# MLP down-projection of a float32 trunk kernel: 2x2 block products with seven multiplications instead of eight, and buffers that start at multiples of 256 bytes

## The chip, the core and the metric

The kernel runs on one core of a Trainium2 chip. A core has TensorE (PE in the profile; PEld is its weight load), VectorE (DVE), ScalarE (ACT), GpSimd (POOL) and a queue that issues transfers (SP). SBUF is its on-chip memory of 128 partitions, PSUM the eight banks (128 partitions x 512 float32) that matmuls add into. The metric is the device time of one execution in microseconds; lower is better. Before the change it is 1307.33 us, the median of three runs between 1307.11 and 1307.74.

## The reference, cut to what matters

Two residual layers (a gated position mixer, then forgetting attention), each followed by a squared-ReLU MLP, on 512 tokens of width 1024, all in float32. The change touches the MLP, which runs twice:

```python
D_MODEL = 1024; SEQ = 512; D_FF = 4 * D_MODEL
def sqrelu_mlp(h, w1, w2):
    return jnp.square(jax.nn.relu(h @ w1)) @ w2
for i in range(DEPTH):                      # DEPTH = 2
    x = x + mixer(rms_norm(x, mix_norm_g[i]))
    x = x + sqrelu_mlp(rms_norm(x, mlp_norm_g[i]), mlp_w1[i], mlp_w2[i])
```

## The kernel before, in words

The residual stream lies transposed in SBUF as eight tiles `x0` to `x7`, each 128 features x 512 tokens. A float32 operand is split into a rounded high part and the remainder (`fp32r` tiles: `wh`, `wl` of a weight, `xh`, `xl` of the normed stream, `zh`, `zl` of the hidden values), and one product is three matmuls (`mm3`, line 198): high by high, high by low, low by high. All matmuls of the page stand at line 191, the helper `mm`.

Weights come through `Stream` (line 46): 512 KB chunks of 128 x 1024, loaded by SP into one of three `raw` buffers (line 65), split by ACT (`wh`, line 75) and by DVE or, in the attention stage, POOL (`wl`, line 77), into four `wh` and four `wl` buffers. `take` (line 91) hands out the next chunk and splits three chunks further ahead. The order of the instructions on each engine is made by a scheduler from the program's order, except in the attention stage, whose matmuls are pinned.

An MLP (`mlp`, from line 397) works in eight groups of four 128-wide blocks of the 4096 hidden features. `up` (`dense_a`, line 256) makes one hidden block: 8 input blocks x 3 = 24 matmuls of 512 columns into a PSUM bank `ph`. `square` turns it into `zh`, `zl`: DVE takes the ReLU and the row scale (`r`, line 409), ACT squares (`z`, line 411) and rounds (`zh`, line 414), DVE subtracts (`zl`, line 415). `out_chunk` (line 278) then takes a 256-column chunk of `w2` for the four hidden blocks of the *previous* group: 2 output blocks x 4 x 3 = 24 matmuls of 512 columns into banks `po`, each followed by an add into `x` on DVE (line 273). So `up` and `out_chunk` alternate, 24 matmuls each, and POOL has no work in an MLP. At the end of each MLP four `out_chunk` follow each other. In the second MLP each finished `x` is stored; in the first it goes into the attention stage's norm (`Norm.block`, line 213).

Where the buffers lie: in the built program, `raw`, `wh`, `wl`, `x`, `xh`, `xl` and the gated mixer's `zh`, `zl` (`gzh`, `gzl`) start 64 bytes past a multiple of 256 in their partition, the MLP's `zh`, `zl` 192 past one, the attention stage's `oh`, `ol` 128 or 64 past one.

Of the kernel before, what the change touches and what calls it, by code (L numbers as in the profile page):

```python
# [8 lines left out]
F32 = mybir.dt.float32  # L9
F32R = mybir.dt.float32r  # L10
AF = mybir.ActivationFunctionType
ALU = mybir.AluOpType
# [4 lines left out]
P = 128  # L17
# [25 lines left out]
WARM = 20  # L43


class Stream:


    def __init__(self, nc, pool, chunks, bufs, ahead, load_ahead, halved=()):
        self.nc, self.pool, self.chunks, self.bufs = nc, pool, chunks, bufs  # L50
# [7 lines left out]

    def _load(self):
        i = self.loaded  # L60
        src = self.chunks[i]
# [5 lines left out]
        self.loaded += 1  # L67

    def _split(self):
        nc, i = self.nc, self.split  # L70
        t, n = self.raw.pop(i)
        hi = self.pool.tile([P, CHUNK_COLS], F32R, tag="wh", name=f"wh{i}", bufs=self.bufs[1])
        lo = self.pool.tile([P, CHUNK_COLS], F32R, tag="wl", name=f"wl{i}", bufs=self.bufs[1])
        for sl in self._pieces(i, n):
            nc.scalar.activation(hi[:, sl], t[:, sl], AF.Copy)  # L75
            eng = nc.gpsimd if i in self.pooled else nc.vector
            eng.tensor_tensor(lo[:, sl], t[:, sl], hi[:, sl].bitcast(F32), op=ALU.subtract)  # L77
        self.parts[i] = (hi, lo)
        self.split += 1

    def load(self, upto):
        while self.loaded < min(len(self.chunks), upto):
# [16 lines left out]
def trunk(ctx: ExitStack, tc: tile.TileContext, A, out, stages=4):  # L99
# [30 lines left out]

    def mlp_chunks(w1, w2):
        r = []
        for g in range(8):
            for m in range(4):
                r += [w1[4 * g + m], w2[g - 1, m]] if g else [w1[4 * g + m]]
        return r + [w2[7, m] for m in range(4)]

    chunks += mlp_chunks(A["m0_1"], A["m0_2"])
    lo_pool = [len(chunks)]
# [40 lines left out]
    dve.memset(mhalf, -0.5)  # L180

# [5 lines left out]
            tc.keep_in_program_order(ins)  # L187
            order["us"] += max(cols, 256) / 2400

    def mm(dst, a, b, start, stop):  # L190
        ins = pe.matmul(dst, a, b, start=start, stop=stop)  # L191
        placed(ins, dst.shape[-1])
        return ins

    def turn(dst, src):
        placed(pe.transpose(dst, src, ident[: src.shape[0], : src.shape[0]]), 256)

    def mm3(dst, ah, al, bh, bl, start, stop, pin=False):
        first = mm(dst, ah, bh, start, False)
        if pin:  # L200
            tc.keep_in_program_order(first)
        mm(dst, ah, bl, False, False)
        mm(dst, al, bh, False, stop)

    class Norm:

# [87 lines left out]
    with ExitStack() as st:  # L294
        gp = st.enter_context(tc.tile_pool(name="gp", bufs=1))

        v = [gp.tile([P, E], F32, tag=f"v{i}", name=f"v{i}") for i in range(NT)]
        bn = small.tile([P, NT, 4, 6], F32, tag="bn", name="bn")
        for g in range(4):
# [18 lines left out]
            if g == 1:  # L318
                wsT = wp.tile([P, G, P], F32, tag="raw", name="wsT", bufs=3)
                nc.sync.dma_start(wsT, A["w_sT"].rearrange("g s t -> s g t"))  # L320
                pool.affine_select(wsT, wsT, pattern=[[0, G], [1, P]], compare_op=ALU.is_ge, fill=0.0, base=0, channel_multiplier=-1)
                wsb = gp.tile([P, G, 2, P], F32R, tag="wsb", name="wsb")
                pool.tensor_scalar(wsb[:, :, 0], wsT, 1.0, None, op0=ALU.mult)
                pool.tensor_tensor(wsb[:, :, 1], wsT, wsb[:, :, 0].bitcast(F32), op=ALU.subtract)
                lngb = gp.tile([P, 2, E // P], F32, tag="lngb", name="lngb")
                nc.sync.dma_start(lngb, A["ln_gb"])
# [68 lines left out]


    def mlp(nm, done):
        with ExitStack() as st:
            mp = st.enter_context(tc.tile_pool(name="mp", bufs=2))
            prev = None  # L400
# [5 lines left out]
            def square(f, ph):  # L406
                f = f"{nm.n}_{f}"
                r = mp.tile([P, S], F32, tag="r", name=f"r{f}", bufs=2)
                dve.scalar_tensor_tensor(r, ph, 0.0, nm.rbc, op0=ALU.max, op1=ALU.mult)  # L409
                z = mp.tile([P, S], F32, tag="z", name=f"z{f}", bufs=2)  # L410
                act.activation(z, r, AF.Square)
                h = mp.tile([P, S], F32R, tag="zh", name=f"zh{f}", bufs=8)
                l = mp.tile([P, S], F32R, tag="zl", name=f"zl{f}", bufs=8)
                act.activation(h, z, AF.Copy)
                dve.tensor_tensor(l, z, h.bitcast(F32), op=ALU.subtract)
                return h, l

            for g in range(8):
                if g == 0:
                    phs = [up(0), up(1)]  # L420
                    nm.finish()
                    phs.append(up(2, True))
                    nm.spread()
                    phs.append(up(3, True))
                    z = [square(f, ph) for f, ph in enumerate(phs)]
                else:
                    z = []
                    for m in range(4):
                        z.append(square(4 * g + m, up(4 * g + m)))
                        out_chunk(m, *prev, 4, 256)  # L430
                zh, zl = ([t[q] for t in z] for q in range(2))
                prev = (zh, zl)
            out_partial(*prev, 4, 256, done)

    def store(b):
        nc.sync.dma_start(out[b * P : (b + 1) * P, :], x[b])
# [11 lines left out]

    nx3 = Norm(3)
    with ExitStack() as st:  # L450
        fp = st.enter_context(tc.tile_pool(name="fp", bufs=2))
        qkg = fp.tile([P, 2], F32, tag="qkg", name="qkg", bufs=1)
        nc.scalar.dma_start(qkg, A["qk_g"])
        qkn = fp.tile([P, 1], F32, tag="qkn", name="qkn", bufs=1)
        dve.tensor_scalar(qkn, qkg[:, 0:1], -(DH**-0.5), None, op0=ALU.mult)
        bf = fp.tile([P, H], F32, tag="bf", name="bf", bufs=1)
        nc.sync.dma_start(bf, A["b_f"].partition_broadcast(P))
        tri = fp.tile([P, P], F32, tag="tri", name="tri", bufs=1)
        pool.affine_select(tri, ones, pattern=[[1, P]], compare_op=ALU.is_ge, fill=0.0, base=0, channel_multiplier=-1)
        did = set()  # L460
# [72 lines left out]
        def project(p, values=True):  # L533
# [26 lines left out]
            ss = fp.tile([P, NT, 4], F32, tag="yss", name=f"yss{p}")  # L560
# [39 lines left out]
        def attend(p, y):  # L600
# [21 lines left out]
            for e in range(2):  # L622
# [6 lines left out]
                sm = fp.tile([P, NT], F32, tag="sm", name=f"sm{hd}")  # L629
                mn = fp.tile([P, NT], F32, tag="mn", name=f"mn{hd}")  # L630
# [16 lines left out]
                rc = fp.tile([P, NT], F32, tag="rc", name=f"rc{hd}")  # L647
# [170 lines left out]
```

## Time and profile before

| | before |
|---|---|
| median of three runs | 1307.33 us |
| the profiled execution's own time | 1307.18 us |
| its span, first to last instruction | 1305.5 us |
| PE busy | 1294.8 us (99%), 6196 matmuls |
| DVE busy | 742.0 us (57%) |
| ACT busy | 547.4 us (42%) |
| POOL busy | 309.0 us (24%) |

The profiled execution is 0.15 us below the median; 1.7 us of it lie around the span. A matmul's row in the timeline has a modelled end, so the pace of matmuls is read from one start to the next, or from the chain of work that ended last, which merges a run of them: 24 matmuls and the time to the next piece. A busy share is an average over stages; the MLPs fill about 287 to 640 us and 955 to 1302 us.

### The profile page before, as it was taken

What the parts mean: (1) busy time and instruction counts of PE and PEld (TensorE: products, weight loads), DVE (VectorE), ACT (ScalarE), POOL (GpSimd) and SP (SyncE); (2) the same over time, 40 slices, a digit from 0 to 9 for tenths busy, and PEclk for the clock granted to TensorE, in tenths of its full rate; (3) what the DMA queues carried; (4) which work ended last, traced back from release to release, by engine and by line L of the source; (5) the groups of instructions that cost most, each with busy time, mean ns of one, the idle gap of its engine ahead of it and who ended that gap; (6) DMA issues with size and microseconds to landing.
All of it is one profiled execution on the core that took longest, in us unless ns stands there. A gap on an engine that the chain in (4) does not pass through costs nothing. (4 is left out here: it accounts for less than half of the span.)

```text
span 1305.5 us, 16106 instructions
## 1 busy us (share of the span) xinstructions
PE 1294.8 (99%) x6196; PEld 1090.5 (84%) x6196; DVE 742.0 (57%) x1132; ACT 547.4 (42%) x864; POOL 309.0 (24%) x296
## 2 busy tenths in 40 slices
PE   9999999999999999999999999999999999999998
PEld 8888888888888888888899899998878888888886
DVE  7347766684444444444637777777864444444443
ACT  7234332343333333222467687787443332222231
POOL 4108523020000000000657567675320000000000
PEclk9999999999999999999999999999999999999999
DMA  7332322323333333332223222223222322333321
GB/s 243 97 111 84 87 91 86 92 90 94 95 93 97 97 97 97 97 97 93 70 87 102 82 81 78 93 67 112 82 87 92 96 97 97 97 98 97 97 81 65
DMA packets 39485, 123.87 MB, mean 95 GB/s; under 512 B 4688, under 2 KB 5728, under 8 KB 39408
## 3 DMA queue, kind: packets, MB, share of 16 engines
q1 hardware_dynamic: 39232, 122.82, 30.1%
q8 instruction: 49, 0.80, 0.2%
q14 instruction: 28, 0.23, 0.1%
q0 software_dynamic: 32, 0.02, 0.0%
q10 hardware_dynamic: 144, 0.00, 0.0%
HBM read 120.69 MB, written 2.13 MB: 94 GB/s over the span
## 5 line engine op out<-in xcount | busy, mean ns | idle before, releaser
L75 ACT ACTIVATE wh<-raw 128x1024 fp32r<-128x1024 f32 (+3 forms) x230 | 231.9, 1008 | 599.9 <-PE ph L191 264.5
L77 DVE TENSOR_TENSOR wl<-raw,wh 128x1024 fp32r<-128x1024 f32 (+1 forms) x178 | 220.6, 1240 | 78.9 <-ACT wh L75 73.4
L273 DVE TENSOR_TENSOR x<-x,po 128x512 f32<-128x512 f32 x192 | 131.0, 686 | 153.5 <-PE po L191 150.9
L191 PE MATMUL po<-zh,wl 128*128 128x512 f32 x512 | 202.2, 395 | 0.0
L191 PE MATMUL po<-zl,wh 128*128 128x512 f32 x512 | 202.0, 394 | 0.0
L191 PE MATMUL po<-zh,wh 128*128 128x512 f32 x512 | 201.8, 395 | 0.0
L191 PE MATMUL ph<-xl,wh 128*128 128x512 f32 x512 | 199.5, 390 | 0.7 <-DVE xl L219 0.7
L191 PE MATMUL ph<-xh,wh 128*128 128x512 f32 x512 | 199.6, 390 | 0.0
L191 PE MATMUL ph<-xh,wl 128*128 128x512 f32 x512 | 199.4, 390 | 0.0
L77 POOL TENSOR_TENSOR wl<-raw,wh 128x768 fp32r<-128x768 f32 (+3 forms) x52 | 102.4, 1970 | 398.2 <-ACT wh L75 395.7
L409 DVE SCALAR_TENSOR_TENSOR r<-ph,rbc 128x512 f32<-128x512 f32 x64 | 44.1, 692 | 187.5 <-PE ph L191 187.3
L191 PEld LDWEIGHTS po<-zl,wh 128*128 128x128 f32 x512 | 96.1, 188 | 23.2
L191 PEld LDWEIGHTS po<-zh,wl 128*128 128x128 f32 x512 | 96.1, 188 | 23.2
L191 PEld LDWEIGHTS po<-zh,wh 128*128 128x128 f32 x512 | 96.1, 188 | 22.6
L191 PEld LDWEIGHTS ph<-xl,wh 128*128 128x128 f32 x512 | 96.1, 188 | 21.6 <-DVE xl L219 1.4
L191 PEld LDWEIGHTS ph<-xh,wh 128*128 128x128 f32 x512 | 96.1, 188 | 20.7
L191 PEld LDWEIGHTS ph<-xh,wl 128*128 128x128 f32 x512 | 96.1, 188 | 20.2
L191 PE MATMUL pq<-wh,xh 128*128 128x384 f32 (+2 forms) x256 | 88.7, 347 | 0.0
L191 PE MATMUL pq<-wh,xl 128*128 128x384 f32 (+2 forms) x256 | 83.4, 326 | 0.0
L191 PE MATMUL pq<-wl,xh 128*128 128x384 f32 (+2 forms) x256 | 83.2, 325 | 0.0
L355 POOL TENSOR_SCALAR vn<-v,mv,lnr 128x128 f32<-128x128 f32 x64 | 65.1, 1029 | 57.6 <-DVE vl L359 57.5
L191 PE MATMUL pv<-wh,xh 128*128 128x512 f32 (+1 forms) x160 | 58.8, 372 | 0.0
(154 smaller groups left out, 2180.9 us busy)
## 6 DMA issues: line engine op xcount, KB each, us to landing
raw<-in_m_dram SPq DMA_DIRECT2D x128, 512.0 KB, 3.6
raw<-in_gw_u_dram SPq DMA_DIRECT2D x16, 512.0 KB, 3.5
raw<-in_gw_o_dram SPq DMA_DIRECT2D x16, 512.0 KB, 3.5
raw<-in_fw_qkv_dram SPq DMA_DIRECT2D x20, 384.0 KB, 3.0
raw<-in_gw_v_dram SPq DMA_DIRECT2D x14, 512.0 KB, 3.6
raw<-in_fw_g_dram SPq DMA_DIRECT2D x8, 512.0 KB, 3.6
cb<-cd SPq DMA_DIRECT2D x16, 256.0 KB, 3.3
raw<-in_fw_o_dram SPq DMA_DIRECT2D x8, 512.0 KB, 3.6
```

The lines of the kernel that those rows point to most:

```text
L75: nc.scalar.activation(hi[:, sl], t[:, sl], AF.Copy)
L77: eng.tensor_tensor(lo[:, sl], t[:, sl], hi[:, sl].bitcast(F32), op=ALU.subtract)
L191: ins = pe.matmul(dst, a, b, start=start, stop=stop)
L273: dve.tensor_tensor(x[b], x[b], pt, op=ALU.add)
L355: pool.tensor_scalar(vn[:, i], v[i][:, cb * P : (cb + 1) * P], mv[:, i, 0:1], lnr[:, i : i + 1], op0=ALU.subtract, op1=ALU.mult)
L409: dve.scalar_tensor_tensor(r, ph, 0.0, nm.rbc, op0=ALU.max, op1=ALU.mult)
```

## The change: seven products, and where buffers lie

The down-projection's hidden features are taken in four groups of 1024 instead of eight of 512. In a group, an output of 256 features x 512 tokens is a 2x2 block matrix: the weights are blocks A11, A12, A21, A22 (output halves by hidden halves; A11 and A21 come in the first `w2` chunk, A12 and A22 in the second) and the hidden values are blocks B11, B12, B21, B22 (hidden halves by token halves, 256 tokens each). Four sums of each are made beforehand: `_sums` makes S1 = A21 + A22, S2 = S1 - A11, S3 = A11 - A21, S4 = A12 - S2 on POOL (128x512 each), split by ACT and DVE (128x1024, twice); `squares` makes T1 = B12 - B11, T2 = B22 - T1, T3 = B22 - B12, T4 = B21 - T2 on POOL (128x256 each), and one ACT round and one DVE subtract over seven of the eight blocks (128x1792). Then come seven products of 4 x 3 matmuls of 256 columns. Their intermediate results are chained in PSUM: a bank is added into `x` by DVE, and PE then goes on adding into the same bank:

```python
product(a, a11, B11, z, True);   add(b1, late, a)
product(c, s1, T1, z, True);     add(b2, early, c)
if behind: behind()              # the previous pair's last product
product(a, s2, T2, z, False);    add(b1, early, a)
product(b, a12, B21, z, True);   add(b1, late, b)
product(c, s4, B22, z, False);   add(b1, early, c)
product(a, s3, T3, z, False);    add(b2, early, a)
# later, as `last`: product(a, a22, T4, z, False); add(b2, late, a)
```

A pair of chunks (one `down`) is thus 84 matmuls of 256 columns, where the two `out_chunk`s over the same weights were 48 of 512 columns; an MLP has 16 pairs. `add` is seven DVE adds of 128x256 for a pair. The order in an MLP is no longer one `up` and one `out_chunk` in turn:

```diff
+MLP_ORDER = [("up", 0, n) for n in range(4)]
+for _g in range(4):
+    MLP_ORDER += [("up", _g + 1, 0)] if _g < 3 else []
+    MLP_ORDER += [("down", _g, n) for n in range(4)]
+    MLP_ORDER += [("up", _g + 1, n) for n in range(1, 4)] if _g < 3 else []
...
+        if kind == "first":
+            self._parts(*(blocks(q)[:, :, 0] for q in (hi, lo, t)), eng)
...
+        s = sp.tile([P, 4, h], F32, tag="ssum", name=f"ssum{i}", bufs=1)
...
+        tt(s1, a21, a22, op=ALU.add)
+        tt(s2, s1, a11, op=ALU.subtract)
+        tt(s3, a11, a21, op=ALU.subtract)
+        tt(s4, a12, s2, op=ALU.subtract)
...
+            hi = sp.tile([P, 2, h], F32R, tag="sh", name=f"sh{i}_{q}", bufs=3)
+            lo = sp.tile([P, 2, h], F32R, tag="sl", name=f"sl{i}_{q}", bufs=3)
+            self._parts(hi, lo, s[:, 2 * q : 2 * q + 2], nc.vector)
...
+    def pad(at, words):
+
+        dve.memset(at.tile([P, words], F32, tag="pad", name="pad", bufs=1), 0.0)
...
+    pad(const, 48)
...
+            pad(mp, 32)
...
-            for g in range(8):
...
-                        z.append(square(4 * g + m, up(4 * g + m)))
-                        out_chunk(m, *prev, 4, 256)
```

Here an `up` is a pair of hidden blocks (48 matmuls of 512 columns). The `pad` tiles and small tiles that moved to pools of their own (`fs` in the attention stage, `lngb` ahead of the mixer's other tiles) put every operand of a matmul at a multiple of 256 bytes. Up to the first MLP every engine's instructions stand in the order that they had, the load of `lngb` in SP's queue too; only the memsets of the pads are new on DVE.

On PE, at the end of the second MLP's last `up` (`ph3_31` is the bank of hidden block 31), the down-projection began with hidden blocks 24 to 27, which were long done:

```order
L191 MATMUL ph3_31_10698<-xl3_7_8544,wh222_10593 128x512
L191 MATMUL ph3_31_10698<-xh3_7_8543,wl222_10594 128x512
L191 MATMUL po224_0_10739<-zh3_24_10222,wh223_10628 128x512
L191 MATMUL po224_0_10739<-zl3_24_10223,wh223_10628 128x512
L191 MATMUL po224_0_10739<-zh3_24_10222,wl223_10629 128x512
L191 MATMUL po224_0_10739<-zh3_25_10295,wh223_10628 128x512
```

Now thirty matmuls on the hidden values `zh3_3_0` and `zh3_3_1` of the same group follow `ph3_31` (banks `ca` and `cc` of pairs 0 and 1 and `cb` of pair 0); these are the last of them, and then those that need `zh3_3_2`:

```order
L243 MATMUL cc3_3_1_12134<-zh3_3_0_11287,sl223_0_12004 128x256
L243 MATMUL cc3_3_1_12134<-zh3_3_1_11825,sh223_0_12003 128x256
L243 MATMUL cc3_3_1_12134<-zl3_3_1_11826,sh223_0_12003 128x256
L243 MATMUL cc3_3_1_12134<-zh3_3_1_11825,sl223_0_12004 128x256
L243 MATMUL ca3_3_0_12017<-zh3_3_2_11900,wh220_11863 128x256
L243 MATMUL cc3_3_0_12031<-zh3_3_2_11900,sh221_0_11916 128x256
L243 MATMUL cb3_3_0_12058<-zh3_3_2_11900,wh221_11907 128x256
```

The hidden values of the group's last `up` (`zh3_3_3`, the blocks of `ph3_31`) are needed 45 matmuls behind `ph3_31`, their low part 50 behind it.

On DVE, in the middle of the first MLP, an `out_chunk` and an `up` in turn asked this of it (`po` adds, weight splits `wl`, the ReLU `r`, the hidden `zl`):

```order
L273 TENSOR_TENSOR x0_97<-x0_97,po62_0_2965 128x512
L273 TENSOR_TENSOR x1_98<-x1_98,po62_1_2979 128x512
L77 TENSOR_TENSOR wl65_2997<-raw65_2886,wh65_2996 128x1024
L409 SCALAR_TENSOR_TENSOR r1_9_3024<-ph1_9_2993,rbc1_2563 128x512
L77 TENSOR_TENSOR wl66_3035<-raw66_2921,wh66_3034 128x1024
L415 TENSOR_TENSOR zl1_9_3029<-z1_9_3026,zh1_9_3028 128x512
```

Now, between two `down`s of one group, adds for three banks of two pairs stand among splits of weights and of weight sums (`sl`):

```order
L88 TENSOR_TENSOR wl79_3749<-raw79_3597,wh79_3748 128x1024
L490 TENSOR_TENSOR x0_97<-x0_97,ca1_1_0_3665 128x256
L88 TENSOR_TENSOR sl77_1_3656<-ssum77_3646,sh77_1_3655 128x1024
L490 TENSOR_TENSOR x0_97<-x0_97,cc1_1_0_3679 128x256
L490 TENSOR_TENSOR x2_99<-x2_99,ca1_1_1_3771 128x256
L490 TENSOR_TENSOR x1_98<-x1_98,ca1_1_0_3665 128x256
L490 TENSOR_TENSOR x2_99<-x2_99,cb1_1_1_3825 128x256
L490 TENSOR_TENSOR x2_99<-x2_99,cc1_1_1_3785 128x256
L88 TENSOR_TENSOR sl79_0_3758<-ssum79_3752,sh79_0_3757 128x1024
```

An add into `x` stood behind work on other tiles before too, but PE had two more banks to go on with; now PE's next product into the same bank waits for that add.

More of the change, by code (lines that the diff above doesn't have):

```diff
@@ L43, with blocks @@
 WARM = 20
+MLP_ORDER = [("up", 0, n) for n in range(4)]
[3 more added lines that the diff above has]
+    MLP_ORDER += [("up", _g + 1, n) for n in range(1, 4)] if _g < 3 else []
+def blocks(t):
+    return t.rearrange("p (k o m) -> p k o m", k=4, o=2)
 class Stream:
     def __init__(self, nc, pool, chunks, bufs, ahead, load_ahead, halved=()):
-        self.nc, self.pool, self.chunks, self.bufs = nc, pool, chunks, bufs
+        self.nc, self.pool, self.bufs = nc, pool, bufs
+        self.chunks = [c if isinstance(c, tuple) else (c, None) for c in chunks]
+        self.sums_pool = None
         self.ahead, self.load_ahead = ahead, load_ahead
@@ L67, in _load, with _parts, _sums @@
         self.loaded += 1
+    def _parts(self, hi, lo, t, eng):
+        self.nc.scalar.activation(hi, t, AF.Copy)
+        eng.tensor_tensor(lo, t, hi.bitcast(F32), op=ALU.subtract)
     def _split(self):
         nc, i = self.nc, self.split
-        t, n = self.raw.pop(i)
+        kind = self.chunks[i][1]
+        t, n = self.raw[i] if kind == "first" else self.raw.pop(i)
         hi = self.pool.tile([P, CHUNK_COLS], F32R, tag="wh", name=f"wh{i}", bufs=self.bufs[1])
         lo = self.pool.tile([P, CHUNK_COLS], F32R, tag="wl", name=f"wl{i}", bufs=self.bufs[1])
[L74 to L77, printed above, removed]
+        eng = nc.gpsimd if i in self.pooled else nc.vector
+        if kind == "first":
+            self._parts(*(blocks(q)[:, :, 0] for q in (hi, lo, t)), eng)
+        for sl in self._pieces(i, n) if kind != "first" else []:
+            self._parts(hi[:, sl], lo[:, sl], t[:, sl], eng)
         self.parts[i] = (hi, lo)
+        if kind == "second":
+            self._sums(i, self.raw.pop(i - 1)[0], t)
         self.split += 1
+    def _sums(self, i, f, g):
+        nc, sp = self.nc, self.sums_pool
+        h = CHUNK_COLS // 2
+        a11, a12, a21, a22 = (blocks(t)[:, :, o] for o in range(2) for t in (f, g))
+        s = sp.tile([P, 4, h], F32, tag="ssum", name=f"ssum{i}", bufs=1)
+        tt = nc.gpsimd.tensor_tensor
+        s1, s2, s3, s4 = (s[:, q].rearrange("p (k m) -> p k m", m=P) for q in range(4))
+        tt(s1, a21, a22, op=ALU.add)
+        tt(s2, s1, a11, op=ALU.subtract)
+        tt(s3, a11, a21, op=ALU.subtract)
+        tt(s4, a12, s2, op=ALU.subtract)
+        made = []
+        for q in range(2):
+            hi = sp.tile([P, 2, h], F32R, tag="sh", name=f"sh{i}_{q}", bufs=3)
+            lo = sp.tile([P, 2, h], F32R, tag="sl", name=f"sl{i}_{q}", bufs=3)
+            self._parts(hi, lo, s[:, 2 * q : 2 * q + 2], nc.vector)
+            made += [tuple(t[:, e].rearrange("p (k m) -> p k m", m=P) for t in (hi, lo)) for e in range(2)]
+        self.parts[i] += (made,)
     def load(self, upto):
@@ L132, in mlp_chunks @@
         r = []
-        for g in range(8):
-            for m in range(4):
-                r += [w1[4 * g + m], w2[g - 1, m]] if g else [w1[4 * g + m]]
-        return r + [w2[7, m] for m in range(4)]
+        for kind, g, n in MLP_ORDER:
+            if kind == "up":
+                r += [w1[8 * g + n], w1[8 * g + 4 + n]]
+            else:
+                r += [(w2[2 * g, n], "first"), (w2[2 * g + 1, n], "second")]
+        return r
     chunks += mlp_chunks(A["m0_1"], A["m0_2"])
@@ L188, in placed, with mm @@
             order["us"] += max(cols, 256) / 2400
-    def mm(dst, a, b, start, stop):
-        ins = pe.matmul(dst, a, b, start=start, stop=stop)
+    def mm(dst, a, b, start, stop, more=False):
+        ins = pe.matmul(dst, a, b, start=start, stop=stop, skip_group_check=more)
         placed(ins, dst.shape[-1])
@@ L196, in turn, with mm3 @@
         placed(pe.transpose(dst, src, ident[: src.shape[0], : src.shape[0]]), 256)
-    def mm3(dst, ah, al, bh, bl, start, stop, pin=False):
-        first = mm(dst, ah, bh, start, False)
+    def mm3(dst, ah, al, bh, bl, start, stop, pin=False, more=False):
+        first = mm(dst, ah, bh, start, False, more)
         if pin:
             tc.keep_in_program_order(first)
-        mm(dst, ah, bl, False, False)
-        mm(dst, al, bh, False, stop)
+        mm(dst, ah, bl, False, False, more)
+        mm(dst, al, bh, False, stop, more)
     class Norm:
@@ L295, in trunk @@
         gp = st.enter_context(tc.tile_pool(name="gp", bufs=1))
+        lngb = gp.tile([P, 2, E // P], F32, tag="lngb", name="lngb")
+        nc.sync.dma_start(lngb, A["ln_gb"])
         v = [gp.tile([P, E], F32, tag=f"v{i}", name=f"v{i}") for i in range(NT)]
@@ L397, in mlp @@
     def mlp(nm, done):
+        HS = S // 2
+        early, late = slice(0, HS), slice(HS, S)
         with ExitStack() as st:
             mp = st.enter_context(tc.tile_pool(name="mp", bufs=2))
-            prev = None
+            ws.sums_pool = mp
+            pad(mp, 32)
             def up(f, pin=False):
@@ L404, in up @@
                 return ph
[L406 to L415, printed above, removed]
-                return h, l
@@ L418, in mlp, with squares @@
-            for g in range(8):
-                if g == 0:
-                    phs = [up(0), up(1)]
+            def squares(name, phs):
+                c = mp.tile([P, 8, HS], F32, tag="zc", name=f"zc{name}", bufs=1)
+                for e, ph in enumerate(phs):
+                    v = c[:, 2 * e : 2 * e + 2].rearrange("p a n -> p (a n)")
+                    dve.scalar_tensor_tensor(v, ph, 0.0, nm.rbc, op0=ALU.max, op1=ALU.mult)
+                    act.activation(v, v, AF.Square)
+                b12, b11, b22, b21, t1, t2, t3, t4 = (c[:, q] for q in range(8))
+                pool.tensor_tensor(t1, b12, b11, op=ALU.subtract)
+                pool.tensor_tensor(t2, b22, t1, op=ALU.subtract)
+                pool.tensor_tensor(t3, b22, b12, op=ALU.subtract)
+                pool.tensor_tensor(t4, b21, t2, op=ALU.subtract)
+                h = mp.tile([P, 7, HS], F32R, tag="zh", name=f"zh{name}", bufs=4)
+                l = mp.tile([P, 7, HS], F32R, tag="zl", name=f"zl{name}", bufs=4)
+                act.activation(h, c[:, 1:], AF.Copy)
+                dve.tensor_tensor(l, c[:, 1:], h.bitcast(F32), op=ALU.subtract)
+                return h, l
@@ new lines, in mlp, with product, add, down @@
+            B11, B22, B21, T1, T2, T3, T4 = range(7)
+            first = {0: True}
+            def product(dst, w, q, z, start):
+                wh, wl = w
+                for k in range(4):
+                    ah, al, bh, bl = wh[:, k], wl[:, k], z[k][0][:, q], z[k][1][:, q]
+                    mm3(dst, ah, al, bh, bl, start and k == 0, k == 3, more=not start)
+            def add(b, half, src):
+                dve.tensor_tensor(x[b][:, half], x[b][:, half], src, op=ALU.add)
+            def down(g, n, z, behind):
+                b1, b2 = 2 * n, 2 * n + 1
+                wa, wb = ws.take(), ws.take()
+                a11 = tuple(blocks(t)[:, :, 0] for t in wa)
+                a12, a22 = (tuple(blocks(t)[:, :, o] for t in wb[:2]) for o in range(2))
+                s1, s2, s3, s4 = wb[2]
+                name = f"{nm.n}_{g}_{n}"
+                a = psA(f"ca{name}")[:, :HS]
+                product(a, a11, B11, z, True)
+                add(b1, late, a)
+                c = psB(f"cc{name}")[:, :HS]
+                product(c, s1, T1, z, True)
+                add(b2, early, c)
+                if behind:
+                    behind()
+                product(a, s2, T2, z, False)
+                add(b1, early, a)
+                b = psB(f"cb{name}")[:, :HS]
+                product(b, a12, B21, z, True)
+                add(b1, late, b)
+                product(c, s4, B22, z, False)
+                add(b1, early, c)
+                product(a, s3, T3, z, False)
+                add(b2, early, a)
+                if g == 3 and done:
+                    done(b1)
+                def last():
+                    product(a, a22, T4, z, False)
+                    add(b2, late, a)
+                    if g == 3 and done:
+                        done(b2)
+                return last
@@ L421, in mlp @@
+            zs = {}
+            behind = None
+            for kind, g, n in MLP_ORDER:
+                if kind == "down":
+                    behind = down(g, n, [zs[g, k] for k in range(4)], behind)
+                    continue
+                if behind:
+                    behind()
+                    behind = None
+                fs = (8 * g + n, 8 * g + 4 + n)
+                if (g, n) == (0, 0):
+                    phs = [up(fs[0]), up(fs[1])]
                     nm.finish()
-                    phs.append(up(2, True))
+                elif (g, n) == (0, 1):
+                    more = [up(fs[0], True)]
@@ L423, in mlp @@
                     nm.spread()
-                    phs.append(up(3, True))
-                    z = [square(f, ph) for f, ph in enumerate(phs)]
-                else:
-                    z = []
-                    for m in range(4):
-                        z.append(square(4 * g + m, up(4 * g + m)))
-                        out_chunk(m, *prev, 4, 256)
-                zh, zl = ([t[q] for t in z] for q in range(2))
-                prev = (zh, zl)
-            out_partial(*prev, 4, 256, done)
+                    more.append(up(fs[1], True))
@@ L435, in store @@
+                    zs[0, 0] = squares(f"{nm.n}_0_0", phs)
+                    zs[0, 1] = squares(f"{nm.n}_0_1", more)
+                    continue
+                else:
+                    phs = [up(f) for f in fs]
+                if (g, n) != (0, 0):
+                    zs[g, n] = squares(f"{nm.n}_{g}_{n}", phs)
+            behind()
     def store(b):
@@ L628, in attend @@
                 ees = []
[L629 to L630 removed]
+                sm = fs.tile([P, NT], F32, tag="sm", name=f"sm{hd}")
+                mn = fs.tile([P, NT], F32, tag="mn", name=f"mn{hd}")
                 for i in range(NT):
```

16 lines of the change are left out of this document (8 added, 8 removed).

## The prediction

> **What bounds the kernel now.** I read the page first: its span and its engine rows.
>
> ```profile
> span 1305.5 us, 16106 instructions
> PE 1294.8 (99%) x6196; PEld 1090.5 (84%) x6196; DVE 742.0 (57%) x1132; ACT 547.4 (42%) x864; POOL 309.0 (24%) x296
> ```
>
> PE is busy from end to end. The waits of PE, longest in total first, are small:
>
> ```profile
> PE tp L196 <- DVE ptl L685: 2.8, 3, 1.9
> PE warm L165 <- DVE mhalf L180: 1.1, 1, 1.1
> ```
>
> So the kernel is its matmuls, and the pace of a matmul is the price of everything. The chain that ended last gives that pace in the second MLP (start, us, what):
>
> ```profile
> 997.39 5.59 PE po L191 x24
> 1002.98 5.46 PE ph L191 x24
> 1008.44 5.59 PE po L191 x24
> ```
>
> A `po` matmul takes 5.59/24 = 232.9 ns, a `ph` matmul 5.46/24 = 227.3 ns, both of 512 columns. What the other engines do in the same stretch stands in the windows view (us, then busy PE, PEld, DVE, ACT, POOL, clock, DMA):
>
> ```profile
> 1100.00:1200.00 100.00, 100.00 (x436) 81.55 (x435) 46.92 (x55) 29.54 (x36) 0.00 (x0) 1.00 0.31 96
> ```
>
> DVE is half idle in an MLP, POOL wholly; the clock is full. That idle time is what the change spends.
>
> **What it removes on PE.** The groups by shape give the counts:
>
> ```profile
> L191 PE MATMUL po<-zh,wl 128*128 128x512 f32 x512 | 202.2, 395 | 0.0
> L191 PE MATMUL ph<-xh,wh 128*128 128x512 f32 x512 | 199.6, 390 | 0.0
> L191 PE MATMUL pq<-wh,xh 128*128 128x384 f32 x160 | 58.1, 363 | 0.0
> L191 PE MATMUL po<-gzh,wh 128*128 128x512 f32 x128 | 50.2, 396 | 0.0
> L191 PE MATMUL pu<-xh,wh 128*128 128x512 f32 x128 | 50.0, 391 | 0.0
> L191 PE MATMUL pv<-wh,xh 128*128 128x512 f32 x128 | 49.5, 392 | 0.0
> L191 PE MATMUL pg<-xh,wh 128*128 128x512 f32 x64 | 26.4, 413 | 0.0
> L191 PE MATMUL po<-oh,wh 128*128 128x512 f32 x64 | 26.2, 409 | 0.0
> ```
>
> Each row is one of three alike. The down-projections are 3 x 512 = 1536 matmuls: 1536 x 232.9 = 357.7 us. They become 2 MLPs x 16 pairs x 84 = 2688 matmuls of 256 columns. The trace has such matmuls, each with its own weight load, in the attention stage:
>
> ```profile
> 891.82 0.28 PE L191 MATMUL pv<-wh,xl 128*128 128x256 f32 x1
> ...
> 894.34 0.28 PE L191 MATMUL pv<-wh,xl 128*128 128x256 f32 x1
> 894.46 0.22 PE L191 MATMUL lg<-ks,qs 128*128 128x128 f32 x1
> 894.51 0.28 PE L191 MATMUL lg<-kl,qs 128*128 128x128 f32 x1
> 894.63 0.33 PE L191 MATMUL pv<-wh,xh 128*128 128x256 f32 x1
> 894.80 0.28 PE L191 MATMUL pv<-wl,xh 128*128 128x256 f32 x1
> ```
>
> From 891.82 to 894.34 start 21 more: 2.52/21 = 120 ns each. So 2688 x 120 = 322.6 us, and PE does 35.1 us less. One eighth of the columns would be 44.7 us; the rest goes to a fixed part per matmul, which more, shorter matmuls pay more often. Bounds: half of a `po` (116.5 ns) gives -44.7; if each of the 224 products began with a gap as from 894.63 to 894.80 (170 ns, 50 more), -24.
>
> The weight loads speak against short matmuls:
>
> ```profile
> L191 PEld LDWEIGHTS pv<-wh,xh x160: 187/188/192, 7.2 to 902.6; 128*128 128x128 f32 x160
> ```
>
> A load lasts 188 ns, longer than the 120. If loads could not overlap each other, the products would take 2688 x 188 = 505 us and the kernel 147 us more; the run at 120 ns excludes it. [...]
>
> **Where buffers start.** `ph` reads its moving operand from 64 bytes past a multiple of 256, `po` from 192 past one, otherwise alike: 227.3 against 232.9 ns, some 2.8 ns for each 64 bytes. Carried on to 0 this is 224.5 ns, 2.8 less for the 3 x (512 + 3 x 128 + 2 x 64) = 3072 other matmuls of 512 columns: -8.6. For the 480 of 384 columns I take 2 ns, -1.0; for the new products half, 1.4 ns, -3.8. Sum -13.4. No row starts at 0, so the ends are far apart. At one end starts don't matter: 0. At the other, the whole fixed part goes: from 120 ns at 256 columns to 227.3 at 512 a column costs 0.42 ns, which leaves 12 ns over 512 x 0.42, and the two 128-column starts above, 0.05 us apart, leave almost none over 128 x 0.42 = 54. I take the value near the two rows that differ in the start alone.
>
> **What it adds on DVE and POOL.** Durations in the MLP of before (1000 to 1260 us), and of POOL's adds:
>
> ```profile
> L77 DVE TENSOR_TENSOR wl<-raw,wh 128x1024 fp32r<-128x1024 f32 x47 | 57.6, 1226 | 8.2 <-ACT wh L75 8.2
> L273 DVE TENSOR_TENSOR x<-x,po 128x512 f32<-128x512 f32 x48 | 33.0, 688 | 51.7 <-PE po L191 50.7
> L415 DVE TENSOR_TENSOR zl<-z,zh 128x512 fp32r<-128x512 f32 x24 | 16.6, 692 | 0.0
> L75 ACT ACTIVATE wh<-raw 128x1024 fp32r<-128x1024 f32 x47 | 49.9, 1061 | 181.2 <-PE ph L191 101.1 <-PE po L191 80.1
> L414 ACT ACTIVATE zh<-z 128x512 fp32r<-128x512 f32 x23 | 14.6, 633 | 0.7
> L411 ACT ACTIVATE z<-r 128x512 f32<-128x512 f32 x23 | 14.3, 621 | 0.0
> L233 POOL TENSOR_TENSOR sqs<-sqs,sq x24: 1291/1623/2156, 11.0 to 953.0; 128x512 f32<-128x512 f32 x24
> ```
>
> DVE pays 1.04 ns a column ((1226 - 692)/512) and 0.16 us an instruction. One `down` (84 x 120 ns = 10.1 us of PE) asks of it 0.69 + 1.23 (`wl`), 2 x 1.23 (`sl`) and 7 adds of 256 columns at 0.42 = 2.9: 7.3 us. POOL, undisturbed 1.29 us a sum (the least in its row), has 4 sums: 5.2 us. Each fits beside 10.1. But the two get in each other's way:
>
> ```profile
> 627.10 2.41 POOL L77 TENSOR_TENSOR wl<-raw,wh 128x1024 fp32r<-128x1024 f32 x1 [325.57 <-ACT wh L75]
> 627.67 2.38 DVE L219 SCALAR_TENSOR_TENSOR xl<-x,gains,xh 128x512 fp32r<-128x512 f32 x1 [0.79 <-ACT xh L218]
> 629.47 1.75 POOL L233 TENSOR_TENSOR sqs<-sq,sq 128x512 f32<-128x512 f32 x1
> 631.44 0.75 DVE L219 SCALAR_TENSOR_TENSOR xl<-x,gains,xh 128x512 fp32r<-128x512 f32 x1 [0.80 <-ACT xh L218]
> ```
>
> The first `xl` takes 2.38 us where the second, alone, takes 0.75: it ends 0.5 us behind POOL's `wl`, and POOL's next add takes 1.75 for 1.29. So a DVE instruction with two SBUF inputs and a POOL add take turns. Of a `down`'s 7.3 us on DVE 4.4 are such; only the 2.9 of adds from PSUM can run beside POOL. The pair needs between 4.4 + 5.2 = 9.6 us and 12.5 us for 10.1 us of PE. In the `up`s there is room: a pair of hidden blocks (48 x 227.3 ns = 10.9 us of PE) asks four half-width steps of POOL, 0.65 each if half of 1.29. And about one pair of weights is made ahead.
>
> What queues behind: a DVE split that waits for POOL holds up the adds behind it, and PE's next product into the same bank waits for the add. PE goes from one product to another bank's in between (1.4 us each), which covers a turn or so. I charge 2 us for each of the eight blocks of four `down`s: +16, between 0 and 48.
>
> SP's loads now wait for POOL too: a first chunk's buffer comes free after three sums (3.9 us), and the load behind it lands 3.6 us later:
>
> ```profile
> raw<-in_m_dram SPq DMA_DIRECT2D x128, 512.0 KB, 3.6
> ```
>
> That is 7.5 us a pair below 10.1; with two DVE turns let in it is 10, so it costs nothing alone. ACT (some 4 us a `down`) has room. The pads' memsets on DVE (four) lie under PE's work.
>
> **The end of each MLP.** Behind the last `up` the new order lets PE run 45 matmuls (5.4 us) before it needs that `up`'s hidden values. These take an add-and-scale (0.69), a square (0.62), three of POOL's half-width steps (2.0), a round of 1792 columns (0.63 + 1280 x (1061 - 633)/512 ns = 1.7) and a subtract (2.0): 5.0 us to the high part, 7.0 to the low, which is needed after 6.0, all without turns. With two or three turns I take 3 us for each MLP: +6, between 2 and 12. Before, this work lay under the next chunk.
>
> **Sum.** -35.1 - 13.4 + 16 + 6 = -26.5 us on the profiled execution's 1307.2: 1280.7; the median of the runs of before is 0.15 above that execution. I forecast 1280.
>
> **Rivals.** *Starts matter more.* The fixed 12 ns falls to 3, as in the 128-column pair: -9 x 3072 = -27.6, -9 x 480 = -4.3, and -9 x 2688 = -24.2 in the products, of which I leave half, since 9.3 us of PE for a `down` would be below the pair's 9.6. With the +22: 1307.2 - 35.1 - 27.6 - 4.3 - 12 + 22 = 1250. For it: two stages differ by the start alone. Against it: from 64 to 192 it is worth 5.6, not more. [...]
>
> *DVE and POOL become the bound (slower).* If they take turns throughout, a `down` takes 12.5 us, 2.4 over PE; with the first of each four made ahead, 24 x 2.4 = 58 us; products gain nothing from their starts: 1307.2 - 35.1 - 9.6 + 58 + 6 = 1326. It decides from (35.1 + 9.6 - 6)/24 = 1.6 us a `down`, 11.7 in all. For it: the rows at 627 us. Against it: PSUM adds are 40% of DVE's part. [...]
>
> *Starts don't matter at all*, and `po` differs from `ph` for another reason: that part of the change does nothing, 1307.2 - 35.1 + 22 = 1294.
>
> **Chances.** Forecast 0.45 (own range 1262 to 1290), starts idle 0.15, starts worth more 0.27, DVE and POOL bound 0.13. The range 1226 to 1304 takes in three of them, with the far end of the starts, and leaves out the fourth and a small tail below. A measurement of this kernel tells 0.2%, 2.6 us, from no change. Faster 0.85, same 0.03, slower 0.12.
>
> **What would show it.** Right: product matmuls 118 to 120 ns apart; `ph` at 224 to 225; PE's waits some 20 us, for DVE's adds and for `sl`, in the blocks of `down`s and behind the last `up`. Wrong: `ph` at 227 or below 220; PE waits over 50 us, with DVE's `sl` far above 1.23 us; products over 130 ns apart without a wait.

## The result: slower, and the profile after

| | before | after |
|---|---|---|
| median (range), four runs each | 1307.43 us (1307.11 to 1307.74) | 1322.41 us (1318.58 to 1325.16) |
| ratio to before, 95% interval | | 1.0113 [1.0085, 1.0141] |
| the profiled execution's own time, its span | 1307.18, 1305.5 us | 1323.94, 1322.2 us |

The change made the kernel slower by 15 us; the forecast was 1280 and its range ended at 1304. The page of after, engines and two of the rows of 40 slices:

```profile
span 1322.2 us, 18960 instructions
...
PE 1277.0 (97%) x7348; PEld 1138.5 (86%) x7348; DVE 844.6 (64%) x1264; ACT 607.7 (46%) x896; POOL 618.5 (47%) x552
...
PE   9999999999899999997999999999998999999978
...
PEclk9999999999999999997999999999998999999979
```

(Line numbers from here on are those of each kernel: in after `mm` is line 243, weight splits 88, weight sums 113 to 116, the hidden path 467 to 477, the adds 490.) PE has less to do (1277.0 us for 1294.8) in a longer span, and for the first time there are slices in which neither PE nor its clock is full. PE's waits, longest total first:

```profile
PE ca L243 <- ACT zh L476: 27.2, 10, 4.0
...
PE ca L243 <- DVE zl L477: 3.1, 4, 1.2
PE ca L243 <- DVE x L490: 2.3, 2, 1.8
...
PE cc L243 <- DVE x L490: 1.0, 1, 1.0
...
PE cc L243 <- DVE sl L88: 0.3, 1, 0.3
```

The waits that I forecast, for DVE's adds into `x` and for `sl`, are 3.6 us together. What PE waits for is the hidden values: 30.3 us. All of that lies near the starts of blocks of `down`s, where the values of the last `up` pair are needed, and in an MLP's last block those of the pair before it too. Further into a block PE hardly waits, as two stretches of the second MLP show, one at the start of a block and the next inside it (us, then busy PE, PEld, DVE, ACT, POOL, clock, DMA):

```profile
1014.00:1024.00 10.00, 5.95 (x31) 5.75 (x31) 6.17 (x8) 4.17 (x5) 3.51 (x5) 0.66 0.25 83
1024.00:1058.00 34.00, 34.00 (x286) 34.00 (x285) 23.19 (x36) 11.14 (x12) 14.02 (x11) 1.00 0.33 100
```

The path that PE waits for is in the chain that ended last (start, us, what), from one hidden pair of the second MLP to the next and to PE:

```profile
1080.96 0.61 DVE zc L467
...
1082.37 0.74 POOL zc L470
1083.11 1.74 issue
1084.89 1.29 POOL ssum L113
1086.18 0.70 POOL zc L471
...
1092.32 1.93 DVE zl L477
...
1099.00 1.14 POOL zc L470
1100.14 1.25 POOL ssum L114
...
1102.09 0.70 POOL zc L471
1102.79 2.23 POOL ssum L116
1105.02 0.71 POOL zc L473
1105.76 1.70 ACT zh L476
1107.51 0.39 PE ca L243
```

Two things are seen here. POOL's steps for the hidden values (`zc`, lines 470 to 473) stand in its queue in turn with weight sums (`ssum`), which run 1.3 us undisturbed and up to 2.2 here. And the chain runs through more than one pair: `zc` has one buffer, so the next pair's first step has to wait until the last `zl` of the pair before is done. The end of the second MLP shows the second of these; the timeline of DVE there:

```profile
1270.42 2.02 DVE L477 TENSOR_TENSOR zl<-zc,zh 128x1792 fp32r<-128x1792 f32 x1 [3.14 <-ACT zh L476]
1272.48 1.29 DVE L467 SCALAR_TENSOR_TENSOR zc<-ph,rbc 128x512 f32<-128x512 f32 x2
1278.63 2.03 DVE L477 TENSOR_TENSOR zl<-zc,zh 128x1792 fp32r<-128x1792 f32 x1 [4.86 <-ACT zh L476]
```

and of PE, the last `ph` matmul, and what waits:

```profile
1263.36 0.39 PE L243 MATMUL ph<-xh,wl 128*128 128x512 f32 x1
...
1270.44 0.58 PE L243 MATMUL ca<-zh,wh 128*128 128x256 f32 x1 [3.11 <-ACT zh L476]
...
1278.65 0.58 PE L243 MATMUL ca<-zh,wh 128*128 128x256 f32 x1 [3.65 <-ACT zh L476]
```

The last `ph` is done at 1263.75. Its ReLU could run then, but the pair's ReLUs start at 1272.48, 0.04 us behind the `zl` of the pair before; from there the path takes 8.2 us (to 1280.66), not far from what I had worked out (7.0; POOL's four steps take 2.9 us where I had three, 2.0). So the path began 8.7 us late, and little on it was slow. Whether the buffer alone holds its start is what the run with two buffers has to show.

Last, PE's pace. In the chain of before `ph` took 227.3 ns; in that of after still 228, and a product's matmul 120 ns:

```profile
1029.40 2.88 PE ca L243 x24
...
1064.65 5.93 PE ph L243 x26
```

But for a while behind the wait at 1270 products are further apart:

```profile
1282.16 0.41 PE L243 MATMUL ca<-zl,wh 128*128 128x256 f32 x1
...
1286.42 0.35 PE L243 MATMUL cc<-zh,sl 128*128 128x256 f32 x1
```

From 1282.16 to 1286.42 there are 20 matmuls: 213 ns each. The trace's clock record has PE at half its clock from 1269.48 to 1286.55, and four other times in or right behind the waits at a block's start: 44 us in all, in stretches of 3.4, 3.4, 6.8, 13.7 and 17.1 us. What lies ahead of the one that begins at 440.05 is a wait of 2.0 us (436.7 to 438.7).

### The profile page after: what moved, and what is told of

It reads as the page before. It is cut to its first block, busy times and chain, and to the rows that moved or that the text cites. A ratio compares the mean times of both kernels' runs of the same rounds, so it can differ in the third digit from the quotient of the medians.

```text
span 1322.2 us, 18960 instructions
## 1 busy us (share of the span) xinstructions
PE 1277.0 (97%) x7348; PEld 1138.5 (86%) x7348; DVE 844.6 (64%) x1264; ACT 607.7 (46%) x896; POOL 618.5 (47%) x552
## 5 line engine op out<-in xcount | busy, mean ns | idle before, releaser
L87 ACT ACTIVATE wh<-raw 128x1024 fp32r<-128x1024 f32 (+3 forms) x230 | 216.4, 944 | 290.6 <-PE ph L243 71.1
L87 ACT ACTIVATE sh<-ssum 128x1024 fp32r<-128x1024 f32 x64 | 67.6, 1056 | 123.8 <-POOL ssum L114 99.7
L470 POOL TENSOR_TENSOR zc<-zc 128x256 f32<-128x256 f32 x32 | 32.7, 1021 | 191.3 <-ACT zc L468 191.3
L477 DVE TENSOR_TENSOR zl<-zc,zh 128x1792 fp32r<-128x1792 f32 x32 | 67.4, 2107 | 75.2 <-ACT zh L476 75.2
L88 DVE TENSOR_TENSOR sl<-ssum,sh 128x1024 fp32r<-128x1024 f32 x64 | 89.0, 1392 | 39.7 <-ACT sh L87 39.5
L490 DVE TENSOR_TENSOR x<-x,ca 128x256 f32<-128x256 f32 x128 | 52.7, 416 | 87.2 <-PE ca L243 86.8
L243 PE MATMUL ca<-zh,wh 128*128 128x256 f32 x256 | 75.6, 296 | 29.6 <-ACT zh L476 27.2
L476 ACT ACTIVATE zh<-zc 128x1792 fp32r<-128x1792 f32 x32 | 54.3, 1698 | 103.4 <-POOL zc L473 56.6
L113 POOL TENSOR_TENSOR ssum<-raw,raw 128x512 f32<-128x512 f32 x32 | 48.9, 1529 | 90.2 <-DVE sl L88 76.5
L115 POOL TENSOR_TENSOR ssum<-raw 128x512 f32<-128x512 f32 x32 | 49.4, 1544 | 69.4 <-DMA raw<-in_m_dram 69.4
```

Of the source, the lines that this page charges most:

```text
L87: self.nc.scalar.activation(hi, t, AF.Copy)
L88: eng.tensor_tensor(lo, t, hi.bitcast(F32), op=ALU.subtract)
L113: tt(s1, a21, a22, op=ALU.add)
L115: tt(s3, a11, a21, op=ALU.subtract)
L243: ins = pe.matmul(dst, a, b, start=start, stop=stop, skip_group_check=more)
L470: pool.tensor_tensor(t1, b12, b11, op=ALU.subtract)
```

## The account that the experiments are read by

For each kernel I read from the starts of PE's matmuls in the two MLPs: the idle time (what a start is late beyond 227 ns for `ph` and `po`, 120 for a product) and what the matmuls in half-clock stretches took over their pace. One kernel below (no hidden sums) has all the matmuls of the change, 6.1 us idle and none at half clock; its span less 6.1 is 1268.1. Adding idle and half clock to that gives every other span of the kind to within 1 us:

| kernel | idle, us | half clock, us | 1268.1 + both | span |
|---|---|---|---|---|
| after | 40.5 | 13.0 | 1321.6 | 1322.2 |
| after, starts as before | 42.0 | 13.2 | 1323.3 | 1322.5 |
| two `zc` buffers | 33.1 | 4.8 | 1306.0 | 1305.6 |
| hidden sums on DVE | 31.0 | 9.1 | 1308.2 | 1307.8 |
| two `zc`, split in two parts | 26.3 | 4.0 | 1298.4 | 1299.3 |
| the same, hidden sums on DVE | 9.3 | 1.5 | 1278.9 | 1279.6 |
| no weight sums | 8.9 | 0.0 | 1277.0 | 1277.5 |
| no hidden sums | 6.1 | 0.0 | | 1274.2 |

Before has 1.0 us idle and no half clock in its MLPs. So of the change's loss 34 us are waits over the quiet kernel's 6 and 13 us the half clock behind them; what is left for the work alone is 1305.5 - 1.0 = 1304.5 to 1268.1, -36.4, for the -35.1 that I had for the products alone.

## Experiments

**Starts alone.** Before, with the pads and the moved small tiles of the change, and the old down-projection:

```diff
+    pad(const, 48)
...
+            pad(mp, 32)
...
+        pad(fs, 48)
```

> The old down-projection, with every operand of a matmul moved to a multiple of 256 bytes; nothing else. Theory 'a start 64 past a boundary is already as good as 0' (the changed kernel's ph runs at 227 ns from 0 as from 64): only the po matmuls, which started 192 past, gain 233 - 227 = 5.6 ns each, 1536 x 5.6 = 8.6 us: 1298.8. Theory 'starts are worth nothing, po is slower for another reason': 1307, po still 233 ns apart.

1296.37 us (1295.65 to 1296.53), ratio 0.9915 [0.9899, 0.9932]: 10.8 us faster. The chain of this kernel in the second MLP:

```profile
969.66 5.44 PE po L195 x24
975.10 5.44 PE ph L195 x24
980.54 5.44 PE po L195 x24
```

`po`, whose moving operand started 192 bytes past a multiple of 256, now runs at `ph`'s pace, 226.7 ns for 232.9: 1536 x 6.2 = 9.5 of the 10.8 us. `ph` didn't move from its 227 when its start went from 64 to 0. So there is no slope by 64 bytes: a start at 64 or 0 is the same for 512 columns (227 ns) and 192 took 232.9 (these runs don't single out a start at 128). This part of the change is worth 11 us, but only to the matmuls that the other part removes.

**After with the old starts.** The changed kernel without the three pads; zh, zl, sh and sl start 192 past a multiple of 256:

```diff
-    pad(const, 48)
...
-            pad(mp, 32)
...
-        pad(fs, 48)
```

> The seven products with the old starts (64, 192 and 128 past a boundary), the pads left out. Theory 'starts cost only a stretch of 512 columns read from 192 past': products stay at 120 ns and the time within 5 us of the changed kernel's 1322. Rival 'each 64 bytes cost 2.8 ns for 512 columns, half for 256': products at 124 ns, 2688 x 4 = 11 us more, 1333, if PE's waits don't take it up.

1321.93 us (1320.95 to 1324.21), ratio 1.0114 [1.0099, 1.0130]: the same as after. The chain of the block above in this kernel:

```profile
1029.49 2.88 PE ca L242 x24
1032.37 1.42 PE cb L242 x12
```

Products at 192 take 118 to 120 ns, as at 0. In the changed kernel starts are worth nothing.

**Two buffers of unsplit hidden values.** T3 is written over B12, so a buffer is seven blocks and two fit; the work is the same:

```diff
-                c = mp.tile([P, 8, HS], F32, tag="zc", name=f"zc{name}", bufs=1)
+                c = mp.tile([P, 7, HS], F32, tag="zc", name=f"zc{name}", bufs=2)
...
-                pool.tensor_tensor(t3, b22, b12, op=ALU.subtract)
+                pool.tensor_tensor(b12, b22, b12, op=ALU.subtract)
```

> Two buffers for the hidden values before they are split (zc, seven blocks with T3 written over B12), the same work. Theory 'path': PE waits at the start of a block of downs for the last up's hidden values, and these are late because one zc buffer makes a pair of hidden blocks wait until the pair before it is wholly split (the ReLU starts at 1272.48, zl of the pair before ends at 1272.44): two buffers take most of the 37 us of waits away, and most half-clock stretches with them, 1280 to 1295. Theory 'turns': DVE and POOL cannot do the work in the time, whatever the buffers: 1315 to 1325, waits as before.

1307.75 us (1305.21 to 1308.91), ratio 1.0001 [0.9992, 1.0010]: 14.7 us faster than after, between what the two theories said. Idle falls by 7 us and half clock by 8. The single buffer is a part of the cause; with two PE still waits, 12.6 us for the high parts and 9.0 for the low:

```profile
PE ca L243 <- ACT zh L476: 12.6, 10, 3.5
PE ca L243 <- DVE zl L477: 9.0, 10, 1.2
```

What holds the start of the last path now is the order on DVE. The last `ph` of the second MLP is done at 1252.5, and its pair has a buffer (the pair's first ReLU ran at 1247.88), but the second ReLU stands in DVE's queue behind the `zl` of the pair before, whose sums on POOL were not done before 1252.88:

```profile
1254.91 2.79 DVE L477 TENSOR_TENSOR zl<-zc,zh 128x1792 fp32r<-128x1792 f32 x1 [0.23 <-ACT zh L476]
1257.63 0.68 DVE L467 SCALAR_TENSOR_TENSOR zc<-ph,rbc 128x512 f32<-128x512 f32 x1
```

This ReLU starts 5.1 us late, and the last hidden value is there 12.7 us behind the last `ph`, for 16.9 with one buffer. So the second buffer takes off only a part of the delay.

**No weight sums.** S1 to S4 and their splits are left out, and the products read plain weight blocks instead (so the output is another); matmuls, adds and the hidden path are as after:

```diff
-            self._sums(i, self.raw.pop(i - 1)[0], t)
+            self.raw.pop(i - 1)
+            self.parts[i] += (None,)
...
-                s1, s2, s3, s4 = wb[2]
+                s1, s2, s3, s4 = a12, a22, a11, a22
```

> Leaves the sums of the weights out, with their splits: products two, three, five and six use plain blocks of the weights instead; all matmuls stay. POOL then only makes the hidden sums, and DVE loses 2.46 us a down. Theory 'turns': waits of PE vanish, 1270 to 1278. Theory 'path' with one zc buffer: the path gets shorter by the turns only, waits fall to a half or less, 1280 to 1300.

1279.19 us (one run), between the ranges of the two theories (to 1278, from 1280), so the time alone doesn't tell them apart. Still with one `zc` buffer, the waits for hidden values are nearly gone:

```profile
PE ca L244 <- DVE zl L478: 2.4, 2, 1.2
PE ca L244 <- DVE x L491: 2.3, 2, 1.8
PE ca L244 <- ACT zh L477: 1.6, 2, 0.8
```

The path fits under the `up`s when POOL and DVE have no weight sums in between. So it isn't the buffer alone, but the buffer with a path that the weight sums lengthen.

**Waits filled.** Fillers on PE ahead of each block's first product, to see the half clock without the idle time:

```diff
                 a = psA(f"ca{name}")[:, :HS]
+                for _ in range((28, 10, 10, 40)[g] if n == 0 else 0):
+                    mm(a, a11[0][:, 0], z[2][0][:, B11], True, True, True)
                 product(a, a11, B11, z, True)
```

> The changed kernel with 88 filler matmuls of 256 columns per MLP, 176 in all, put ahead of the first product of each block of downs (28, 10, 10 and 40 of them, at 120 ns 3.4, 1.2, 1.2 and 4.8 us); they read the weights and the hidden values of the third pair, write a bank that the first product then starts anew, and count for nothing. They lie in the time in which TensorE waits for the fourth pair. Theory that the idle time alone is the loss (37 us of waits at the starts of blocks, the half clock behind them without weight): as the changed kernel, 1319 to 1325. Theory that each wait of 2 us and more also halves the clock for 3.4 to 17 us behind it, which costs some 14 us beside the waits: 1305 to 1312, with a mean clock of 0.99 or more. If the fillers aren't covered by the waits: up to 21 us more, 1335 to 1343.

1333.45 us (1331.93 to 1337.06), ratio 1.0201 [1.0183, 1.0219]: 11 us slower than after, and so no test of the half clock. The scheduler put the fillers where products on the first three pairs had stood, and in each MLP's last block behind a wait of some 3.7 us for the third pair, so they displaced cover: idle is still 33.1 us and half clock 12.0. With the fillers' 21.1 us the account gives 1334.3 for a span of 1335.3. What the half clock costs rests on the starts counted in the table, not on a run without it.

**Hidden sums on DVE.**

```diff
-                pool.tensor_tensor(t1, b12, b11, op=ALU.subtract)
+                dve.tensor_tensor(t1, b12, b11, op=ALU.subtract)
```

and so for T2 to T4.

> The changed kernel with the four hidden sums of each pair (T1 to T4) on VectorE and not on POOL; the weight sums stay on POOL. Theory that the hidden sums come late because they stand in POOL's queue behind weight sums of 1.3 to 1.6 us: the waits at the starts of blocks fall from 37 us to under 20, 1298 to 1308. Theory that VectorE's own work and the one buffer of unsplit hidden values set the length of a pair's path: 1315 to 1330, with waits of 30 us or more.

1309.57 us (one run), 13 us faster than after though DVE has more to do: just above the first theory's range, and below the second's. The hidden sums on DVE (least/median/most ns):

```profile
L470 DVE TENSOR_TENSOR zc<-zc x32: 409/422/1510, 308.7 to 1259.8; 128x256 f32<-128x256 f32 x32
```

A sum takes 0.42 us here and does not stand behind a weight sum in POOL's queue. PE's waits:

```profile
PE ca L243 <- ACT zh L476: 10.9, 5, 3.2
PE ca L243 <- DVE x L490: 8.4, 6, 2.8
PE ca L243 <- DVE zl L477: 4.7, 4, 1.7
```

Those for hidden values are half of after's (15.6 us for 30.3), but those for adds into `x` have grown from 3.3 us to 9.1 (with the 0.7 of `cc`): the charge that I had feared, on a smaller scale. The buffer is still single, and 31 us of idle stay.

**No hidden sums.** T1 to T4 are left out, the products read plain blocks, and a pair's split goes over four blocks (the output is another); the weight sums are all there:

```diff
-                c = mp.tile([P, 8, HS], F32, tag="zc", name=f"zc{name}", bufs=1)
+                c = mp.tile([P, 4, HS], F32, tag="zc", name=f"zc{name}", bufs=1)
...
-                pool.tensor_tensor(t1, b12, b11, op=ALU.subtract)
...
-            B11, B22, B21, T1, T2, T3, T4 = range(7)
+            B12, B11, B22, B21 = range(4)
+            T1, T2, T3, T4 = range(4)
```

> The changed kernel without the hidden sums T1 to T4 (left out; the products take plain blocks in their place, so the result is another), and with the splits of a pair over four blocks and not seven; the weight sums stay. Theory that the waits at the starts of blocks are the length of a pair's path from its last up to its split values: the path is shorter by the sums (3 to 5 us) and by 1.5 us of the two splits, so nearly all waits go, 1280 to 1290. Theory that the weight sums keep VectorE and POOL busy whatever the hidden path is: over 1300.

1275.86 us (one run), 4 us below the range of the first theory, its mean clock 1.000. No block of `down`s starts with a wait for hidden values; the longest wait in PE's list after the attention's `tp` is the one for the add that ends an MLP, as there was in after:

```profile
PE tp L248 <- DVE ptl L803: 3.3, 4, 1.9
PE ca L243 <- DVE x L487: 2.7, 2, 2.2
```

DVE and POOL are in each other's way here as in after: POOL's weight sums take 1.5 us for their undisturbed 1.3, `sl` on DVE 1303 ns (in after 1365):

```profile
L88 DVE TENSOR_TENSOR sl<-ssum,sh 128x1024 fp32r<-128x1024 f32 x32 | 41.6, 1303 | 28.8 <-ACT sh L87 28.5
...
L114 POOL TENSOR_TENSOR ssum<-ssum,raw 128x512 f32<-128x512 f32 x16 | 24.2, 1514 | 0.6
```

So the weight sums and their turns cost PE next to nothing by themselves (its waits for `sl` are 0.6 us). They cost what they add to the path of the hidden values.

**Split apart.** Two `zc` buffers, and a pair's plain blocks are split at once, with tiles of their own, the four sums later:

```diff
-                act.activation(h, c, AF.Copy)
-                dve.tensor_tensor(l, c, h.bitcast(F32), op=ALU.subtract)
-                return h, l
+                bparts = parts("b", c[:, 4:])
...
+                return bparts + parts("t", c[:, :4])
```

> Two buffers of unsplit hidden values as in the kernel with two of them (1307.75), and the split of a pair in two parts, each with its own high and low tile: the three plain blocks first, without waiting for the sums, then the four sums. All work stays. Theory that the path of the block's last pair sets the waits that are left (25 us and 4 us of half clock): products on plain blocks can start some 5 us earlier and cover the sums, 1284 to 1294. If the waits come from VectorE and POOL taking turns: 1304 to 1312, since two more instructions per pair are issued and no work goes.

1300.72 us (1299.34 to 1304.11), ratio 0.9951 [0.9933, 0.9969]: 7 us better, where I expected 14 to 24. PE now waits for the sums' part:

```profile
PE cc L243 <- DVE zlt L471: 11.7, 10, 1.8
PE cc L243 <- ACT zht L470: 4.3, 6, 0.7
```

POOL's sums were still in turn with weight sums there (least/median/most ns):

```profile
L483 POOL TENSOR_TENSOR zc<-zc x32: 731/1185/1722, 310.5 to 1256.5; 128x256 f32<-128x256 f32 x32
```

**All three together.** The same kernel with T1 to T4 on DVE:

```diff
-                pool.tensor_tensor(t4, b21, t2, op=ALU.subtract)
+                dve.tensor_tensor(t4, b21, t2, op=ALU.subtract)
```

> Two buffers of unsplit hidden values, a pair's split in two parts (plain blocks first), and the hidden sums on VectorE; all work stays. The kernel with the first two of these ran at 1300.72 with 26 us of TensorE idle in the MLPs beyond the pace and 4 us of half clock; without hidden sums the same count was 6 us and none, at 1275.86. Theory that what is left is the path of a block's last pair, on which the sums stand at 4 of 0.74 to 1.7 us on POOL and 4 of 0.42 us on VectorE: 10 to 15 us less, 1286 to 1292. Theory that the two engines taking turns set the path, so that moving 13 us of sums (32 pairs by 4 by 0.42, less what it spares) onto the busier VectorE brings nothing: 1299 to 1306.

1281.30 us (1279.41 to 1281.54), ratio 0.9797 [0.9781, 0.9813]: 19.4 us less, more than the path theory said and wholly against turns. It is the fastest kernel here that does all the work: 26 us under before, 15 under the starts alone. At the end of its second MLP this is the last step of the path, on DVE:

```profile
1240.34 1.23 DVE L471 TENSOR_TENSOR zlt<-zc,zht 128x1024 fp32r<-128x1024 f32 x1 [1.12 <-ACT zht L470]
```

and these are PE's last `ph` and the product that waits for it:

```profile
1233.66 0.39 PE L243 MATMUL ph<-xh,wl 128*128 128x512 f32 x1
...
1241.62 0.39 PE L243 MATMUL cc<-zlt,sh 128*128 128x256 f32 x1 [0.23 <-DVE zlt L471]
```

The last hidden value is there (1241.57) 7.5 us behind the last `ph` (16.9 in after), and PE waits 0.23 us. DVE, the busiest engine beside PE, is at 71% of this span: having it do more was right, since what counted was when, not how much.

**A product that needs no sum first.** In the first `down` of each block A12 x B21 goes ahead of all others:

```diff
+                if n == 0:
+                    product(b, a12, B21, z, True)
                 product(a, a11, B11, z, True)
```

> As the kernel with the sums on VectorE and the split in two parts, and in the first down of each block the product A12 x B21, which needs only plain blocks, is put ahead of all others: 12 matmuls at 120 ns, 1.4 us more for TensorE to do before the first value that needs a sum. Theory of the path: each of the 8 blocks' waits is shorter by up to 1.4 us, 4 to 11 us less than that kernel. If the products on the weight sums or the adds from PSUM are what comes last: no change, within 2 us.

1282.76 us (1279.80 to 1284.20), ratio 0.9810 [0.9795, 0.9824]: no change, within the runs' ranges. There was next to no wait left to cover.

## Why the prediction was wrong, point by point

- **Less work for PE, -35.1: right.** Outside half clock products took 120 ns in after (2.88 us for 24), 118 to 120 with the old starts and 120 in the fastest kernel, each with a weight load of 0.19 us. The work alone is -36.4.
- **Starts, -13.4: the first step that failed.** The step "some 2.8 ns for each 64 bytes. Carried on to 0" drew a line through two rows that differed in their start, 64 and 192, and went on to 0. The line isn't there: 227 at 0 as at 64 (starts alone), products the same at 0 as at 192 (old starts). The term is 0 here; nearly the whole effect, 9.5 of 10.8 us, belonged to `po`, which the change removes, so it was already in the 232.9 ns of the first term. The rival "starts don't matter at all" was true of the changed kernel, not of the kernel before. No run shows the paces that the low end of the range, 1226, would need: 512 columns took 226.7 ns at best and 256 columns 118, and the fastest kernel that does all the work took 1281.30 us.
- **DVE and POOL in each other's way, +16.** I looked for it where PE waits for a bank (3.3 us of waits for adds in all) and in the throughput of a `down`: neither the charge nor the rival, 12.5 us a `down`, took place, and a `down` runs at its 10.1. That the rival's 1326 lies close to the measured 1322 is chance. Turns are there in after (`sl` took 1.21 to 1.23 us with no work of POOL beside it and up to 2.94 with it, where all 224 adds from PSUM took 0.41 to 0.42), but the harm was to the latency of another path.
- **The end of each MLP, +6: the step that mattered most.** "Behind the last `up`", "5.0 us to the high part, 7.0 to the low" counted the path as if it began when `ph` was done. At the end of the second MLP it began 8.7 us later, behind the last `zl` of the pair before, whose POOL steps stood behind weight sums: for the single `zc` buffer, and with two of them still 5.1 us late for the order on DVE. And the same path ends at the start of every block, not only the last: one pair of `up`s (10.9 us) is all that covers it. Blocks' starts cost 34 us over a kernel without those waits, where I had 22 for everything.
- **Half clock, +13: not priced at all.** I had waits of 2 and 3 us in the sum and took each for its own length.
- So -36.4 + 39.5 idle (40.5 less before's 1.0) + 13.0 = +16.1, measured +16.7 on the spans. That the mended kernel lands at my 1280 is chance: in my sum stood 13 us of starts that aren't there, and 22 us of waits that it doesn't have.

Shown: the hidden pair's path sets the waits (taking it away, or shortening it in three ways, moves the time by 13 to 47 us), and the weight sums count through that path. Argued from the trace, not isolated by a run: the 13 us of half clock as separate from the waits, and how the late start divides between the buffer and the order on DVE outside the pair shown.

## What to carry to other kernels

When a change puts a new intermediate between two matmul stages, work out the latency from the last input to the first use, with its buffer count (when may this begin?) and with what stands ahead of each step in each engine's queue, and set it against the matmuls in between; an engine's busy share says nothing of it. If the path is too long, a second buffer, a shorter first part and the engine that is faster at the step (0.42 us a hidden sum on DVE for 0.73 on POOL) belong together: here they brought 15, 7 and 19 us in that order, and the first alone only came back to the time of before. Waits on TensorE may cost more than their own length: here 40 us of idle had 13 us of half clock beside them. And an effect that belongs to instructions which the change removes can't be won twice.

## What the runs showed of the hardware

- A 512-column fp32r matmul whose moving operand starts 192 bytes past a multiple of 256 took 232.9 ns, at 0 and 64 it took 227; with 256 columns 118 to 120 ns at 0 and at 192.
- In the MLPs of after the clock stood at half in five stretches, of 3.4, 3.4, 6.8, 13.7 and 17.1 us. Each of the six products that started 2.4 us or more late had such a stretch under way or beginning within 1.0 us, and one that started 2.0 us late (at 438.7) had one beginning 1.3 us later; those 1.3, 1.8, 2.0 (at 651.8) and 2.1 us late (at 526.3) had none. At half clock a product's matmul took 213 ns for 120, not twice as long.
- Undisturbed, a 128x256 subtract between SBUF tiles took 0.42 us on DVE and 0.73 on POOL.
